# A decoder layer with expert retrieval: split products for the first block, two heads beside the last projection, another order at the close of blocks 2 and 1

## The chip, the cores and the metric

The kernel runs on one core of one Trainium2 chip. The metric is device time in microseconds (us) of one launch. The kernel before took 1467.91 us (median of 3 runs, 1463.35 to 1468.68). A measurement of it can tell about 0.5% from no change.

## The reference, cut to what matters

A layer on 512 tokens of width 1024, in float32: one projection to q, k, v of two groups of eight heads (dilated windows "a", stick-breaking "b"), an output projection, a layer norm, then a retrieval of 128 single-neuron experts per token out of 16384, and a second norm.

```python
def hybrid_mixer(x, w_in, w_out):
    proj = x @ w_in                       # (512,1024) @ (1024,3072)
    qa, ka, va, qb, kb, vb = split(proj)
    oa = dilated_window_attention(rotary(qa), rotary(ka), va)
    ob = stick_breaking_attention(qb, kb, vb)
    return concat(oa, ob) @ w_out

def stick_breaking_attention(q, k, v):    # per block of 128 queries
    z = q @ k.T * scale
    later = exclusive_reverse_cumsum(where(causal, log_sigmoid(-z), 0))
    return where(causal, exp(log_sigmoid(z) + later), 0) @ v

def peer_ffn(x, ...):                     # 128 experts per token
    idx, gates = top_k_of_products(x)
    act = gates * gelu(x . expert_u[idx])
    return act @ expert_v[idx]

x = layer_norm(alpha * x + hybrid_mixer(x))
x = layer_norm(alpha * x + peer_ffn(x))
```

## The kernel before

The tokens stand in four blocks of 128, tb = 0 to 3. Block 0 goes first by itself, so that its experts can be fetched while the other blocks are still in the mixer; blocks 1 to 3 follow together.

**Block 0.** `project_block0` (L247) runs over six groups of output columns (`GROUPS`, L225: kA, half of v, qA, kB, qB, the other half of v), four weight tiles of 512 KB each. A tile lands in one of four buffers (`WBUF`, name `w`) of the pool `wst` from SP's queue, and is multiplied in plain float32 (L267). Its heads, `four_a` (L423 to L439) and `four_b` (L447 to L462), four heads to a call, are written out by hand between the projection's steps, in a `manual_schedule` block: there each engine gets its instructions in the order of the code. `first_out`, `normalize`, `query_first` and the routing follow.

**Gathers.** With the routing of a block known, 128 rows of an expert table, one per token, are fetched by an indirect DMA that POOL issues (L792), 512 KB each. On DVE one pass forms the dot products (L801, into `hg`) for table u, or adds the scaled rows (L812) for table v. After the last u row of a block comes a Gelu on ACT (L803), which needs another function table than Exp and Ln do.

**The mixed stage.** `project_in` (L280) computes all six groups for blocks 1 to 3 with split products: `wload` copies a weight tile rounded to fp32r on ACT (`high`, L120), takes the remainder on DVE (`low`, L124), and `mm3` (L126 to L129) adds three fp32r products in place of one float32 product. These steps, the gathers (`early`, the first `PRE0` = 72) and the dilated heads of blocks 1 to 3 (`heads_a`) are interleaved in the ratio `MIXB` = (6, 4, 4): six gathers, four projection steps, four head steps. Here a scheduler of the tile framework sets the order.

**The stick-breaking heads.** A loop written by hand runs over 24 tasks, the heads of block 3, then 2, then 1. `head_b` has steps: scores and mask (L352, L354), exponentials on ACT (L358, L360), a running product on DVE (L362), the cumulative sum as a matmul (L364, L366), the last exponential (L368), output (L372). In each pass the loop steps three heads, takes two or three gathers (`take`), and moves a generator `fill` twice: the output projection of the block before (`project_out`, L550) and its norm (`normalize`, with transposes L173 and copies L578). After the loop it finishes what is left in `after` (closing of a block's heads) and `fill`, then runs `project_out(1)`, `normalize(1)`, the queries and the routing of blocks 1 to 3.

**The rest.** Blocks 2 and 3 compute with all experts' weights streamed from memory by SP (L910 and L1207 on PE), while the gathers for blocks 0 and 1 go on.

## Time and profile before

| what | value |
|---|---|
| median of the runs | 1467.91 us |
| the profiled execution's own time | 1464.93 us |
| its span | 1463.2 us |
| mean granted clock of PE | 0.974 of full |
| PE busy | 1364.4 us, 93% |
| DVE busy | 1198.9 us, 82% |
| ACT busy | 514.4 us, 35% |
| POOL busy | 689.6 us, 47% |
| bytes moved | 495.92 MB, 339 GB/s on average |

The page cuts the span into 40 slices of 36.6 us. The first 1.5 slices hold block 0's projection and heads, slices 4 to 8 the mixed stage, slices 9 to 12 the stick-breaking heads and the closing of blocks 2 and 1, the next three the queries and the routing, and the rest the streamed experts and the tail. A row of the timeline gives start, duration, engine, line, what is written and read, the number of instructions in the row, and in brackets the idle time ahead of it with what ended that time. A matmul's end is modelled, so rows of PE overlap by some tenths of a microsecond.

### The profile page before, as it was taken

What the parts mean: (1) busy time and instruction counts of PE and PEld (TensorE: products, weight loads), DVE (VectorE), ACT (ScalarE), POOL (GpSimd) and SP (SyncE); (2) the same over time, 40 slices, a digit from 0 to 9 for tenths busy, and PEclk for the clock granted to TensorE, in tenths of its full rate; (3) what the DMA queues carried; (4) which work ended last, traced back from release to release, by engine and by line L of the source; (5) the groups of instructions that cost most, each with busy time, mean ns of one, the idle gap of its engine ahead of it and who ended that gap; (6) DMA issues with size and microseconds to landing.
All of it is one profiled execution on the core that took longest, in us unless ns stands there. A gap on an engine that the chain in (4) does not pass through costs nothing.

```text
span 1463.2 us, 19573 instructions
## 1 busy us (share of the span) xinstructions
PE 1364.4 (93%) x6642; PEld 1110.5 (76%) x6642; DVE 1198.9 (82%) x2459; ACT 514.4 (35%) x1029; POOL 689.6 (47%) x526
## 2 busy tenths in 40 slices
PE   8997989999989997788899999999999999999796
PEld 4676877767659996667688888888888888888575
DVE  1259989778789999999988877878777887788887
ACT  1322444364422111699922222222222222222342
POOL 0002577677554332104566665555555565556200
PEclk9999999999889999899999999999999999999998
DMA  8778899899889988659899999999999999999872
GB/s 297 257 268 282 305 347 315 297 385 346 282 305 374 328 287 300 222 178 310 277 389 410 409 410 409 410 409 410 409 409 410 409 409 410 409 409 399 332 246 87
DMA packets 162579, 495.92 MB, mean 339 GB/s; under 512 B 15376, under 2 KB 47520, under 8 KB 162480
## 3 DMA queue, kind: packets, MB, share of 16 engines
q0 software_dynamic: 74304, 270.13, 49.1%
q1 hardware_dynamic: 86448, 218.92, 40.7%
q10 hardware_dynamic: 1728, 5.64, 1.0%
q8 instruction: 52, 0.85, 0.2%
q14 instruction: 47, 0.39, 0.1%
HBM read 477.78 MB, written 16.84 MB: 338 GB/s over the span
## 4 chain that ended last, share of the span: by engine, by line
PE 37%; DMA 26%; DVE 25%; issue 7%; ACT 4%; POOL 2%; SPq 0%; DVEq 0%; POOLq 0%; ACTq 0%
DMA g<-peer_v,eidx 15%; PE y L1207 9%; PE h L910 9%; DMA g<-peer_u,eidx 8%; DVE x L812 3%; DVE yg L812 3%; PE m L267 2%; POOL g L792 2%; DVE o L867 2%; PE m L550 2%; PE tr L550 1%; ACT o L876 1%; DVE vl L124 1%; DMA v<-peer_v 1%; DVE g L801 1%
## 5 line engine op out<-in xcount | busy, mean ns | idle before, releaser
L792 POOL DMA_INDIRECT g<-peer_u,eidx x256 | 349.4, 1365 | 325.5 <-DVE topi L597 123.8
L792 POOL DMA_INDIRECT g<-peer_v,eidx x256 | 334.3, 1306 | 348.1 <-DVE x L812 111.4
L910 PE MATMUL h<-xf,w 128*128 128x256 f32 x2048 | 474.0, 380 | 0.0
L910 PEld LDWEIGHTS h<-xf,w 128*128 128x128 f32 x2048 | 384.1, 191 | 52.2
L801 DVE SCALAR_TENSOR_TENSOR g<-g,x 128x1024 f32<-128x1024 f32 x256 | 305.3, 1221 | 44.8 <-DMA g<-peer_u,eidx 44.4
L1207 PE MATMUL y<-vh,a 128*128 128x512 f32 x928 | 287.6, 414 | 9.3 <-ACT a L1193 8.9
L1207 PEld LDWEIGHTS y<-vh,a 128*128 128x128 f32 x928 | 175.1, 190 | 49.7 <-ACT a L1193 11.4
L812 DVE SCALAR_TENSOR_TENSOR x<-g,hg,x 128x1024 f32<-128x1024 f32 x128 | 164.1, 1282 | 24.4 <-DMA g<-peer_v,eidx 23.9
L812 DVE SCALAR_TENSOR_TENSOR yg<-g,hg,yg 128x1024 f32<-128x1024 f32 x126 | 161.6, 1283 | 25.2 <-DMA g<-peer_v,eidx 24.6
L124 DVE TENSOR_TENSOR vl<-v,vh 128x1024 fp32r<-128x1024 f32 x122 | 148.8, 1221 | 36.4 <-ACT vh L1162 36.4
L902 ACT ACTIVATE gl<-h 128x256 f32<-128x256 f32 x128 | 48.6, 380 | 297.3 <-PE h L910 297.2
L1207 PE MATMUL y<-vl,a 128*128 128x512 f32 x464 | 146.4, 397 | 1.1 <-DVE vl L124 1.1
L1162 ACT ACTIVATE vh<-v 128x1024 fp32r<-128x1024 f32 x122 | 128.5, 1053 | 36.0 <-DMA v<-peer_v 18.7
L1207 PEld LDWEIGHTS y<-vl,a 128*128 128x128 f32 x464 | 87.3, 189 | 22.3 <-DVE vl L124 2.5
L1193 ACT ACTIVATE a<-gl 128x512 fp32r<-128x512 f32 x58 | 36.4, 627 | 178.8 <-DVE gl L1187 178.7
L876 ACT ACTIVATE o<-o1b,sg 128x128 f32<-128x128 bf16 x256 | 83.5, 400 | 3.4 <-DVE o1b L861 3.2
L882 PEld LDWEIGHTS m<-o,o 128*128 128x128 f32 x304 | 37.7, 191 | 20.9 <-ACT o L876 18.0
L882 PE MATMUL m<-o,o 128*128 128x128 f32 x304 | 41.7, 280 | 11.8 <-ACT o L876 7.6
L267 PE MATMUL m<-w,x0f 128*128 128x256 f32 (+1 forms) x128 | 45.5, 505 | 5.3 <-DMA w<-w_in 5.1
L128 PE MATMUL m<-wl,x2h 128*128 128x512 f32 x96 | 38.8, 404 | 8.3 <-DVE wl L124 8.3
L867 DVE TENSOR_TENSOR o<-sg,c_small 128x512 f32<-128x512 f32 x64 | 43.7, 683 | 2.4 <-PE a L882 2.2
L1186 DVE TENSOR_TENSOR gl<-gl,gt 128x480 f32<-128x480 f32 x64 | 41.8, 652 | 0.0
(297 smaller groups left out, 1815.5 us busy)
## 6 DMA issues: line engine op xcount, KB each, us to landing
w<-uT SPq DMA_DIRECT2D x128, 512.0 KB, 8.5
v<-peer_v SPq DMA_DIRECT2D x128, 512.0 KB, 7.3
w<-w_in SPq DMA_DIRECT2D x47, 512.0 KB, 4.7
gt<-gd SPq DMA_DIRECT2D x15, 960.0 KB, 11.6
w<-peer_wq SPq DMA_DIRECT2D x16, 512.0 KB, 4.6
wq<-peer_wq SPq DMA_DIRECT2D x16, 512.0 KB, 7.5
gd<-stage SPq DMA_DIRECT2D x15, 512.0 KB, 5.2
gd<-stage SPq DMA_DIRECT2D x15, 448.0 KB, 3.9
```

What stands on the lines that cost most here:

```text
L124: nc.vector.tensor_sub(parts[1], src, parts[0].bitcast(F32))
L267: nc.tensor.matmul(ps[:, ch * wd:(ch + 1) * wd], x0f[:, kk], w[:, k], start=kk == 0, stop=kk == KD - 1)
L792: nc.gpsimd.indirect_dma_start(out=u, out_offset=None, in_=a["peer_v" if kind else "peer_u"], in_offset=bass.IndirectOffsetOnAxis(ap=eidx[ ...
L801: nc.vector.scalar_tensor_tensor(u, u, 1.0, x, op0=OP.mult, op1=OP.mult, accum_out=hs[:, j:j + 1])
L812: nc.vector.scalar_tensor_tensor(acc, u, hs[:, j:j + 1], acc, op0=OP.mult, op1=OP.add)
L867: nc.vector.tensor_tensor(hot2[s], gate[tb][1][:, 0, t:t + TG, None].to_broadcast([P, TG, P]), iota[:, None, :].to_broadcast([P, TG, P]), ...
L876: nc.scalar.activation(hot[s][:, j], o1b[:, :, j], AF.Copy, scale=gate[tb][1][:, 1, t + j:t + j + 1])
L882: nc.tensor.matmul(gps[s][:, j * P:(j + 1) * P], o2[:, j], o1[:, j], start=True, stop=True)
L902: nc.scalar.activation(gls[c // 2][:, c % 2], ps[:, :ND], AF.Gelu)
L910: nc.tensor.matmul(hps[c][:, :ND], us[c][:, k], xf[:, k], start=k == 0, stop=k == KD - 1)
L1162: nc.scalar.activation(vsp[c][0], vs[c], AF.Copy)
L1207: nc.tensor.matmul(yps[t][hf], s_, w_[:, hf * 512:(hf + 1) * 512], start=c == 0 and n == 0, stop=c == P - 1 and n == len(terms) - 1)
```

## The change

Four things change. `project_block0` splits the weights of groups 1 to 5 as `wload` does, and block 0's tokens, and multiplies with `mm3`; group 0 stays in plain float32. The splits come two tiles ahead of their use, and their results stand in the buffers of `wsp` or in those that later hold the other blocks' tokens. The two transposed groups come from a new copy of their columns in memory, `w_t`, in 512-wide tiles. The mixed stage runs five groups; the sixth goes into a new block by hand together with the first two stick-breaking heads and eight gathers, and the ratio is (7, 4, 3) with 80 gathers. The loop over heads starts two passes later; after it the closing steps and the projection of block 1 stand ahead of the transposes of block 2. After the Gelu of block 0 the table that holds both Exp and Ln is loaded.

The diff:

```diff
@@ -73,8 +73,9 @@
 TG = 4
 LEAD = 30
 KT = 6
-MIXB = (6, 4, 4)
-PRE0 = 72
+MIXB = (7, 4, 3)
+PRE2 = 8
+PRE0 = 80
 QGATH = 3
 QH = 2
 PRE1 = 7
@@ -245,26 +246,59 @@
         turn(scaled(tb, kind, scale, ps), dst)
 
     def project_block0():
-        late = {}
+        late, raw, cut = {}, {}, {}
         n = 0
+        tiles = [(g, i) for g in range(len(GROUPS)) for i in range(4)]
+        flat = [x_.rearrange("p k t -> p (k t)") for x_ in (xh, xl)]
+        x0p = [x_[:, :D].rearrange("p (k t) -> p k t", k=KD) for x_ in flat]
+
+        def fetch(m):
+            if m >= len(tiles):
+                return
+            g, i = tiles[m]
+            w = raw[m] = wst.tile([P, 2, 512], F32, name="w", bufs=WBUF)
+            src = a["w_t"][g - 3, i] if GROUPS[g][0] == "t" else a["w_in"][g, i]
+            src = src.rearrange("p (k c) -> p k c", k=2)
+            if m == 0:
+                for k in range(2):
+                    (nc.scalar, nc.sync)[k].dma_start(w[:, k], src[:, k])
+                    (nc.sync, nc.scalar)[k].dma_start(x0f[:, 2 * k:2 * k + 2], a["x0T"][:, 2 * k:2 * k + 2])
+                nc.sync.dma_start(x0f[:, 4:], a["x0T"][:, 4:])
+            else:
+                nc.sync.dma_start(w, src)
+
+        def split(m):
+            if not 4 <= m < len(tiles):
+                return
+            w = raw.pop(m)
+            if m % 4 > 1:
+                parts = [x_[:, (m % 4 - 1) * D:(m % 4) * D].rearrange("p (k c) -> p k c", k=2) for x_ in flat]
+                nc.scalar.activation(parts[0], w, AF.Copy)
+            else:
+                parts = high(wsp, w, [P, 2, 512], "w")
+            low(w, parts)
+            cut[m] = parts
+
+        for m in range(2):
+            fetch(m)
         for g, (kind, _, scale) in enumerate(GROUPS):
             dst = target(g, 0)
             ps = bank("mm")
-            wd, kn = (256, 4) if kind == "t" else (512, 2)
             for i in range(4):
-                ch, kq = (i // 2, i % 2) if kind == "t" else (0, i)
-                w = wst.tile([P, kn, wd], F32, name="w", bufs=WBUF)
-                src = a["w_in"][g, i].rearrange("p (k c) -> p k c", k=kn)
-                if g == i == 0:
-                    for k in range(2):
-                        (nc.scalar, nc.sync)[k].dma_start(w[:, k], src[:, k])
-                        (nc.sync, nc.scalar)[k].dma_start(x0f[:, 2 * k:2 * k + 2], a["x0T"][:, 2 * k:2 * k + 2])
-                    nc.sync.dma_start(x0f[:, 4:], a["x0T"][:, 4:])
-                else:
-                    nc.sync.dma_start(w, src)
-                for k in range(kn):
-                    kk = kn * kq + k
-                    nc.tensor.matmul(ps[:, ch * wd:(ch + 1) * wd], x0f[:, kk], w[:, k], start=kk == 0, stop=kk == KD - 1)
+                fetch(n + 2)
+                split(n + 2)
+                for k in range(2):
+                    kk = 2 * i + k
+                    if g == 0:
+                        nc.tensor.matmul(ps, x0f[:, kk], raw[n][:, k], start=kk == 0, stop=kk == KD - 1)
+                    else:
+                        mm3(ps, x0p[0][:, kk], x0p[1][:, kk], cut[n][0][:, k], cut[n][1][:, k], kk == 0, kk == KD - 1)
+                if n in (1, 2):
+                    sl = slice(4 * n - 4, 4 * n)
+                    nc.scalar.activation(x0p[0][:, sl], x0f[:, sl], AF.Copy)
+                    nc.vector.tensor_sub(x0p[1][:, sl], x0f[:, sl], x0p[0][:, sl].bitcast(F32))
+                raw.pop(n, None)
+                cut.pop(n, None)
                 n += 1
                 if n in late:
                     turn(*late.pop(n))
@@ -277,10 +311,11 @@
             else:
                 late[n + (2 if kind == "rot" else 1)] = scaled(0, kind, scale, ps), dst
 
-    def project_in():
+    def project_in(groups):
         tbs = PARTS[1]
         n = len(tbs)
-        for g, (kind, _, scale) in enumerate(GROUPS):
+        for g in groups:
+            kind, _, scale = GROUPS[g]
             dst = target(g, 1)
             pst = None if kind == "t" else [bank("mm") for _ in range(n)]
             wd, kn = (256, 4) if kind == "t" else (512, 2)
@@ -571,6 +606,8 @@
         for sl in halves:
             nc.vector.scalar_tensor_tensor(r[:, sl], r[:, sl], rs, t[1][:, sl], op0=OP.mult, op1=OP.add)
         yield
+        if tb > 1:
+            yield
         for g in range(2):
             tr = transpose4(r[:, g * 512:(g + 1) * 512], "a" if g and tb == 0 else "tr")
             ks = slice(4 * g, 4 * g + 4)
@@ -801,6 +838,8 @@
             nc.vector.scalar_tensor_tensor(u, u, 1.0, x, op0=OP.mult, op1=OP.mult, accum_out=hs[:, j:j + 1])
             if j == P - 1:
                 nc.scalar.activation(hs, hs, AF.Gelu)
+                if tb == 0:
+                    nc.scalar.preload_act_table_set("natural_log_exp_and_others")
                 nc.vector.tensor_scalar_mul(x, x, ALPHA)
             return
         if j == 0:
@@ -933,7 +972,7 @@
         if out is not None:
             gelu(out, hps.pop(out))
 
-    proj = project_in()
+    proj, last = project_in(range(5)), project_in((5,))
     xload = load_x2()
     with tc.manual_schedule():
         def go(steps, n=1):
@@ -993,7 +1032,32 @@
     early = gathers(PRE0)
     until(mix(route_steps(0, 4, 4), head(early, PRE1), (2, 1)), proj, 1)
     run(head(early, 12), head(proj, 8), (3, 2))
-    run(early, proj, chain(*(heads_a(tb, rest) for tb in PARTS[1])), MIXB)
+    run(head(early, PRE0 - PRE1 - 12 - PRE2), proj, chain(*(heads_a(tb, rest) for tb in PARTS[1])), MIXB)
+
+    tasks = [("b", tb, h) for tb in (3, 2, 1) for h in range(NH)]
+    NTASK = len(tasks)
+    live, sts_, after = {}, {}, []
+
+    def begin(j):
+        kind, tb, h = tasks[j]
+        if h == 0:
+            sts_[tb] = group(tb)
+        live[j] = head_b(tb, h, sts_[tb], ("a", "b", "m0", "m1")[j % 4])
+
+    def go(j):
+        if 0 <= j < NTASK:
+            next(live[j])
+
+    with tc.manual_schedule():
+        order = [(0, 0), (), (0,), (1, 1), (), (), (), ()]
+        for todo in order:
+            for j in todo:
+                if j not in live:
+                    begin(j)
+                go(j)
+            next(last)
+            next(early, None)
+        run(last, early)
     qws.close()
     rqs.close()
     xf = open_pool(ctx, "xfp", "right").tile([P, KD, 2 * P], F32, name="xf")
@@ -1026,23 +1090,14 @@
             for _ in head(gs, n):
                 pass
 
-        tasks = [("b", tb, h) for tb in (3, 2, 1) for h in range(NH)]
-        NTASK = len(tasks)
-        live, sts_, after = {}, {}, []
         fill = iter(())
         lo_ = load_out()
-        for i in range(-1, NTASK + 2):
-            def go(j):
-                if 0 <= j < NTASK:
-                    next(live[j])
-
+        run(head(lo_, 2))
+        for i in range(1, NTASK + 2):
             next(lo_, None)
             new = i + 1 < NTASK
             if new:
-                kind, tb, h = tasks[i + 1]
-                if h == 0:
-                    sts_[tb] = group(tb)
-                live[i + 1] = head_b(tb, h, sts_[tb], ("a", "b", "m0", "m1")[(i + 1) % 4])
+                begin(i + 1)
                 go(i + 1)
             go(i)
             for g_ in list(after):
@@ -1050,11 +1105,13 @@
                     after.remove(g_)
             if new:
                 go(i + 1)
-            next(fill, None)
+            if i <= NTASK:
+                next(fill, None)
             go(i - 1)
             go(i - 1)
-            take(3 if 10 <= i < 18 else 2)
-            next(fill, None)
+            take(3 if 10 <= i < 18 or 18 <= i < NTASK and i % 2 else 2 if i <= NTASK else 0)
+            if i <= NTASK:
+                next(fill, None)
             if i >= 2:
                 go(i - 2)
                 kind, tb, h = tasks[i - 2]
@@ -1066,10 +1123,10 @@
                 for c in range(3):
                     load_u(c)
         for g_ in after:
-            for _ in g_:
-                take(2)
-        for _ in fill:
-            pass
+            next(g_)
+            next(fill)
+            next(g_)
+        take(1)
         qs.close()
         up = open_pool(ctx, "up", "left")
         qls = ExitStack()
@@ -1077,7 +1134,11 @@
         rq = open_pool(qls, "rq", "left")
         tops(PARTS[1])
         load_q(0)
-        for _ in project_out(1):
+        po1 = project_out(1)
+        for _ in head(po1, 4):
+            take(1)
+        run(fill)
+        for _ in po1:
             take(1)
         norm = normalize(1)
         next(norm)
@@ -1312,6 +1373,7 @@
         "xT": x.T.reshape(KD, P, S).transpose(1, 0, 2),
         "x0T": x[:P].T.reshape(KD, P, P).transpose(1, 0, 2),
         "w_in": np.stack([by_tile(f["w_in"].reshape(D, 6, 512)[:, g], g) for g in (1, 2, 0, 4, 3, 5)]),
+        "w_t": np.stack([f["w_in"].reshape(4, 2, P, 6, 512)[:, :, :, g].transpose(0, 2, 1, 3).reshape(4, P, 1024) for g in (4, 3)]),
         "w_out": f["w_out"].reshape(4, 2, P, 2, 512).transpose(3, 0, 2, 1, 4),
         "peer_wq": f["peer_wq"].reshape(2, 4, P, 8, 256).transpose(2, 3, 0, 1, 4),
         "skT": f["peer_sub_keys"].reshape(16, P, P).transpose(2, 0, 1),
```

How this moves instructions is seen at three places. The first is ACT in block 0's projection, from the second turned group on; `su` are the heads' score rows, `x2h` and `wh` copies of weight tiles. Before:

```order
L223 ACTIVATE qA_181<-tr 128x512
L429 ACTIVATE su<-su 128x512 x2
L236 ACTIVATE q<-m_227 128x512
L223 ACTIVATE kB<-tr 128x4x128
L435 ACTIVATE su<-a 128x512
L435 ACTIVATE su<-b 128x512
```

With the change, on the same engine and at the same place:

```order
L276 ACTIVATE x2h<-w 128x1024 x2
L224 ACTIVATE qA_225<-tr 128x512
L464 ACTIVATE su<-su 128x512 x2
L121 ACTIVATE wh<-w 128x1024 x2
L237 ACTIVATE q<-m_299 128x512
L276 ACTIVATE x2h<-w 128x1024
L224 ACTIVATE kB<-tr 128x4x128
L470 ACTIVATE su<-a 128x512
L276 ACTIVATE x2h<-w 128x1024
L470 ACTIVATE su<-b 128x512
```

The copies of weight tiles 16 and 17 (`wh`, x2) now stand right behind the exponentials of the dilated heads' scores (L464, which was L429).

The second place is DVE at the end of the mixed stage, where the projection's last remainders (`wl`), the gathers' passes (`g,hg`) and the first running product of the stick-breaking heads (`su<-a,su`) meet. Before:

```order
L378 TENSOR_TENSOR o<-h,rz 128x512
L801 SCALAR_TENSOR_TENSOR g_2168,hg<-g_2168,x_100 128x1024
L801 SCALAR_TENSOR_TENSOR g,hg<-g,x_100 128x1024 x4
L124 TENSOR_TENSOR wl<-w,wh 128x1024 x2
L801 SCALAR_TENSOR_TENSOR g,hg<-g,x_100 128x1024
L801 SCALAR_TENSOR_TENSOR g_2227,hg<-g_2227,x_100 128x1024
L801 SCALAR_TENSOR_TENSOR g_2230,hg<-g_2230,x_100 128x1024
L801 SCALAR_TENSOR_TENSOR g,hg<-g,x_100 128x1024 x2
L124 TENSOR_TENSOR wl<-w,wh 128x1024
L801 SCALAR_TENSOR_TENSOR g,hg<-g,x_100 128x1024 x2
L362 SCALAR_TENSOR_TENSOR su<-a,su 128x512
```

With the change:

```order
L412 RECIPROCAL rz<-z 128x8
L413 TENSOR_TENSOR o<-h,rz 128x512
L125 TENSOR_TENSOR wl<-w,wh 128x1024
L838 SCALAR_TENSOR_TENSOR g,hg<-g,x_100 128x1024 x2
L397 SCALAR_TENSOR_TENSOR su<-a,su 128x512
L125 TENSOR_TENSOR wl<-w,wh 128x1024
L838 SCALAR_TENSOR_TENSOR g,hg<-g,x_100 128x1024
L838 SCALAR_TENSOR_TENSOR g_2313,hg<-g_2313,x_100 128x1024
L397 SCALAR_TENSOR_TENSOR su<-b,su 128x512
L838 SCALAR_TENSOR_TENSOR g,hg<-g,x_100 128x1024
L125 TENSOR_TENSOR wl<-w,wh 128x1024
```

The first running products (L362, now L397) have moved from behind the last remainder to between the four remainders of the last group. Ahead of the last remainder stand 79 gathers' passes, where there were 72; ahead of the streamed experts' first remainder 240, where there were 238.

The third place is PE at the close of the loop over heads: the last head's cumulative sum (`c_tri`, `mones`) and output (`h<-v,su`), the transposes of block 2's normalized rows (`x_100`) and of the closed heads (`o`), and block 1's output projection (`wo`). Before:

```order
L364 MATMUL m_3044<-su,c_tri 128x256
L366 MATMUL m_3044<-su,mones 128x128
L372 MATMUL h<-v,su 128x64 x2
L173 MATMUL tr<-c_ident,x_100 128x128 x8
L372 MATMUL h<-v,su 128x64 x2
L173 MATMUL tr<-c_ident,o 128x128 x4
L550 MATMUL m_3181<-wo_2381,x_2357 128x512 x2
L550 MATMUL m_3181<-wo_2411,x_2357 128x512 x2
```

With the change:

```order
L399 MATMUL m_3197<-su,c_tri 128x256
L401 MATMUL m_3197<-su,mones 128x128
L407 MATMUL h<-v,su 128x64 x4
L174 MATMUL tr<-c_ident,o 128x128 x4
L585 MATMUL m_3307<-wo_2561,x_2537 128x512 x2
L585 MATMUL m_3307<-wo_2563,x_2537 128x512 x2
L585 MATMUL m_3307<-wo_2565,x_2537 128x512 x2
L585 MATMUL m_3307<-wo_2597,x_2537 128x512 x2
L174 MATMUL tr<-c_ident,x_100 128x128 x8
L585 MATMUL tr<-wo_2625,x_2537 128x512 x2
```

The eight transposes of block 2 have moved from between the last head's outputs to the middle of block 1's output projection.

## The prediction

> **What bounds the kernel now.** I read the slices of the page first, to see which engine is full in which stage; then the windows by stage; then the waits of the stages where the engines are not full; and last the timeline of those places. The slices are 36.6 us each.
>
> ```profile
> span 1463.2 us, 19573 instructions
> PE   8997989999989997788899999999999999999796
> DVE  1259989778789999999988877878777887788887
> PEclk9999999999889999899999999999999999999998
> GB/s 297 257 268 282 305 347 315 297 385 346 282 305 374 328 287 300 222 178 310 277 389 410 409 410 409 410 409 410 409 409 410 409 409 410 409 409 399 332 246 87
> ```
>
> From slice 21 on DMA moves 409 to 410 GB/s without a break: that is the second half, where the experts' weights stream. The first half has no such ceiling. One window of the middle and one of the second half show the two limits:
>
> ```profile
> 475.00:500.00 25.00, 25.00 (x157) 23.10 (x157) 25.00 (x96) 3.11 (x7) 9.72 (x11) 1.00 0.93 327
> 750.00:775.00 25.00, 25.00 (x114) 21.23 (x114) 20.94 (x23) 6.37 (x10) 16.53 (x12) 1.00 1.03 410
> PE y L1207 <- ACT a L1193: 0.7, 1, 0.7
> ```
>
> The columns are PE, PEld, DVE, ACT and POOL busy, then clock, DMA share and GB/s. At 475 us PE and DVE are both full. At 750 us PE is full at full clock and DMA is saturated; the third row is the longest wait for data that PE has from 745 to 1340 us, 0.7 us. So nothing ahead of 450 us is absorbed later: the change touches what runs up to about 440 us, and a microsecond gained or lost there moves the end by a microsecond, except that the gathers left over for later cost DVE and DMA time of their own (part G). All terms below stand against the profiled run, 1464.9 us, 3 us under the median of 1467.9 of the runs shown.
>
> **A, block 0's projection.** What the change speeds up is the matmul of a weight tile:
>
> ```profile
> 18.34 13.92 PE L267 MATMUL m<-w,x0f 128*128 128x512 f32 x40
> 81.76 0.40 PE L128 MATMUL m<-wl,x2h 128*128 128x512 f32 x1
> 81.99 0.40 PE L129 MATMUL m<-wh,x2l 128*128 128x512 f32 x1
> ```
>
> The first row is tiles 6 to 13 of the block's 24: 13.92 us, less the 0.17 us by which a modelled end stands over, is 1.72 us a tile. Split products follow each other every 0.23 us (81.76 to 81.99); six make a tile, 1.37 us. Twenty tiles are split, 20 x 0.35 = 7 us if PE alone set the pace. It does not. A raw tile now holds its buffer through its transfer, an ACT copy and a DVE subtraction:
>
> ```profile
> w<-w_in SPq DMA_DIRECT2D x24, 512.0 KB, 4.6
> L120 ACT ACTIVATE wh<-w 128x1024 fp32r<-128x1024 f32 x24 | 25.4, 1058 | 43.1 <-PE m L129 39.0 <-PE m L128 3.9
> L124 DVE TENSOR_TENSOR wl<-w,wh 128x1024 fp32r<-128x1024 f32 x24 | 29.2, 1219 | 0.3 <-ACT wh L120 0.3
> ```
>
> 4.6 + 1.06 + 1.22 = 6.9 us over four buffers is 1.72 us a tile, just what the f32 matmul took. So PE idles 0.35 us a tile instead of working, and nothing is gained while the stream of tiles sets the pace. Behind this stands the order: on ACT and DVE the splits are queued among the dilated heads' operations, and the split of tile 16 comes after the heads' last row:
>
> ```profile
> 33.38 0.82 PE L423 MATMUL a<-kA,qA 64*128 64x128 f32 x5 [0.69 <-ACT qA L223]
> 34.58 0.69 DVE L426 TENSOR_TENSOR su<-a,c_maska 128x512 f32<-128x512 f32 x1 [4.22 <-PE a L423]
> 40.84 0.69 DVE L430 TENSOR_REDUCE z<-su 128x4 f32<-128x512 f32 x1 [0.70 <-ACT su L429]
> 39.02 1.89 PE L267 MATMUL m<-w,x0f 128*128 128x256 f32 x8
> 59.87 1.02 PE L457 MATMUL a<-su,c_tri 128*128 128x512 f32 x2
> ```
>
> The heads' chain runs from 34.58 to 41.5 us (both shifted by about 0.7, since the scores start at 34.1). In front of it DVE waited 4.22 us and nobody cared; now PE's next tile is behind it. Tile 16 started at 39.02; I have it at 42.3. From there to the end of tile 23 (59.87) took 20.9 us, of which split products save some 3: 42.3 + 20.9 - 3 = 60.2, and the clock falls to half behind a gap of 4 us (part D shows the case), which costs another 2 to 3. **A: +3**, between -7 (all of the matmul gain) and +6 (no gain, and the gap and the clock in full).
>
> A page speaks against this part. The Trainium skill, "TensorE: Matmul & The Clock Gate", section "Architectural detail", says that ACT and DVE run their queues strictly in order; so a subtraction behind a head's reduction cannot overtake it, and the sum by that rule is the +3; were the splits free to overtake, it would be the -7. No row here shows an overtaking.
>
> **B, the mixed stage up to the end of the projection of blocks 1 to 3.** A round holds one weight tile; it had six gathers and now has seven, with three head steps instead of four. The last group moves behind the dilated heads, into a block with the first two stick-breaking heads and eight of the gathers. The order on SP stays as it was, so these weights are fetched as early as before; on POOL the eight gathers are issued between the group's tiles.
>
> ```profile
> 195.00 1.22 DVE L124 TENSOR_TENSOR wl<-w,wh 128x1024 fp32r<-128x1024 f32 x1
> 207.17 1.22 DVE L124 TENSOR_TENSOR wl<-w,wh 128x1024 fp32r<-128x1024 f32 x1
> 202.58 1.22 DVE L801 SCALAR_TENSOR_TENSOR g<-g,x 128x1024 f32<-128x1024 f32 x1
> 203.73 1.22 DVE L801 SCALAR_TENSOR_TENSOR g<-g,x 128x1024 f32<-128x1024 f32 x1
> 196.00:292.00 96.00, 91.59 (x494) 70.99 (x494) 81.73 (x162) 39.23 (x88) 65.41 (x46) 0.98 0.89 313
> 291.93 0.39 PE L129 MATMUL m<-wh,x2l 128*128 128x512 f32 x1
> ```
>
> A round takes 12.2 us (195.00 to 207.17), a gather on DVE 1.15 us (202.58 to 203.73). By the instruction order 79 gathers instead of 72 stand ahead of the last subtraction: 7 x 1.15 = 8.1 us more DVE work before the end of the projection, which was at 292.2. DVE is busy 81.7 of 96 us in this stage, so at most 14.3 us are there to take it; PE is idle 4.4 us. Lower end -4: PE's idle time goes. Upper end +8: no cover, because the heads that are left run their chains without projection work beside them and the last group's splits wait behind two heads' rows. DVE at 85% is nearer to the upper end: **B: +6**. These gathers come back in part E and G, where they are no longer to be done.
>
> **C, the start of the stick-breaking heads.** The first head had nothing beside it:
>
> ```profile
> 297.81 1.12 PE L364 MATMUL a<-su,c_tri 128*128 128x512 f32 x2 [2.31 <-DVE su L362]
> 300.00:305.00 5.00, 5.00 (x21) 3.67 (x20) 5.00 (x11) 3.20 (x6) 4.08 (x4) 0.76 1.02 412
> ```
>
> 2.31 us of waiting, some 0.7 us just before it, and a quarter of 5 us lost to the clock: 4.2 us. Now that head's scores and exponentials lie under the last group's matmuls. **C: -4**, 0 if the group itself waits there.
>
> **D, normalizing block 3.** The transposes move one step later, so that they no longer stand on PE ahead of their input:
>
> ```profile
> 372.51 0.66 PE L173 MATMUL tr<-c_ident,x 128*128 128x128 f32 x4 [1.66 <-DVE x L572]
> 373.85 0.96 PE L173 MATMUL tr<-c_ident,x 128*128 128x128 f32 x4 [0.69 <-ACT xf L578]
> 375.00:380.00 5.00, 5.00 (x20) 4.36 (x20) 5.00 (x11) 2.74 (x6) 4.09 (x4) 0.50 0.69 215
> 380.00:385.00 5.00, 5.00 (x23) 4.28 (x22) 3.14 (x6) 2.19 (x6) 3.02 (x4) 0.57 0.95 336
> 384.68 1.94 PE L550 MATMUL m<-wo,xf 128*128 128x512 f32 x4
> ```
>
> The two waits are 2.35 us; the clock of 0.50 and 0.57 behind them loses 2.5 + 2.15 = 4.65 us. Together 7.0; but DVE is full in 375 to 380 too and sets a floor, so I count five of them: the next output projection starts at 379.5 instead of 384.68. **D: -5**, between 0 and -7.
>
> **E, closing blocks 2 and 1.** PE now runs half of block 1's output projection while DVE normalizes block 2, whose transposes come after it.
>
> ```profile
> 405.12 0.56 PE L372 MATMUL h<-v,su 128*128 128x64 f32 x4
> 405.73 1.28 ACT L161 ACT_TABLE_LOAD   x1
> 410.35 1.11 PE L173 MATMUL tr<-c_ident,x 128*128 128x128 f32 x4 [4.67 <-DVE x L572]
> 412.15 1.12 PE L173 MATMUL tr<-c_ident,x 128*128 128x128 f32 x4 [0.69 <-ACT xf L578]
> 414.70 1.11 PE L173 MATMUL tr<-c_ident,o 128*128 128x128 f32 x4 [0.69 <-ACT o L383]
> 410.00:415.00 5.00, 3.28 (x14) 2.69 (x15) 5.00 (x6) 1.79 (x3) 2.28 (x2) 0.50 0.06 6
> 415.61 8.44 PE L550 MATMUL m<-wo,x 128*128 128x512 f32 x16
> 423.88 7.03 PE L550 MATMUL tr<-wo,x 128*128 128x512 f32 x16
> ```
>
> Waits of 4.67 + 0.69 + 0.69 = 6.05 us go; PE's 3.28 us of work at clock 0.50 would be 1.6, and the first half of the projection took 8.44 where the second half, at full clock, 7.03: 1.6 + 1.4 = 3 more. Sum 9. Against it: the tail of the last head (scores to output) still has some 2 us without ordinary matmuls, and half a clock behind it costs 2 to 4. The table loads, four of 1.28 us, lie in these chains on ACT; kept tables take them out, and they are counted in the waits. **E: -7**, between -3 and -10. What is late next is DVE, which from here on is full.
>
> A rule bears on it. The Trainium skill, "TensorE: Matmul & The Clock Gate", sections "HAM oscillation" and "Part 4: PE-mode transpose", allows gaps up to about 3.4 us and does not count transposes as work. The trace agrees as far as it goes: 371 to 374.6 us, 3.6 us with transposes only, was followed by 0.50. By that rule the 2 us at the tail cost nothing and E would be -9.
>
> **G, gathers left.** By the order two gathers fewer remain when the second half begins. A gather's 0.52 MB at 410 GB/s is 1.28 us (an estimate from the rate row); PE is bound there too. **G: -1**, between 0 and -2.6.
>
> **The sum**: 3 + 6 - 4 - 5 - 7 - 1 = -8, that is 1464.9 - 8 = **1457 us**, from 1450 to 1463 with the smaller errors of C to G.
>
> **Rivals.** *R1, the split pays in full:* transfers land faster than 4.6 us, or the heads' rows fit between the splits. For it: PE's work does fall by 7 us, and DVE and ACT are mostly idle up to 34 us. Against it: 1.72 us a tile from the buffers. A = -7, the sum -18: 1447. *R2, the front eats the gains:* A = +6 and B = +8, the sum -3 by themselves; with C at 0, because the last group waits beside the first heads, +1: 1462 to 1466. For it: DVE's 85%, and the strictly interleaved order. Against: the idle 14.3 us. *R3, slower:* block 0's PE stays at half clock from tile 14 to 23. At half clock a split tile takes 2.74 us against 1.72: 10 x 1.02 = 10 us, and the heads' own matmuls between them (9 us busy) add 5 to 9: +15 to +19 on the forecast, 1472 to 1476. It decides if gaps like that before tile 16 repeat in each group; a gap of 0.7 us (33.38) did not do it, one of 3.6 us did, and I expect one long gap only. That the table would be loaded again anyway is ruled out by the order, where no loads stand between the heads' exponentials.
>
> **How the numbers follow.** Forecast 1457: 0.50. R1 0.17, R2 0.25, R3 0.08. The range takes in R1 with its bounds and R2, and leaves out R3 and the far end of R1: 1443 to 1469. Against the median, 0.5%, about what a measurement of this kernel can tell from no change, is 7.3 us, so faster means under 1460.6: R1 and four fifths of the forecast, 0.57. Within 0.5%: R2 and the rest, 0.35. Slower: R3, 0.08.
>
> **What would show it.** A: tile 23's matmuls end at 61 to 63 us (R1: by 54), with a gap of about 4 us around 40 and waits for the splits on PE. B: the last split product of the projection ends near 298 (R1 and a good B: 292 or less). C and D: no waits of over 1 us for DVE at the start of the heads and after block 3's projection, and the clock above 0.9 there. E: the output projection of block 1 starts about 13 us earlier than 415.6, and PE's wait for block 2's normalized rows is gone. G: the second half's windows are the same. Wrong it would be if DVE's queue, not PE's, sets the stages C to E: then the gathers moved ahead show up as DVE time without a gap, and the gains of C to E shrink to the 2 us of G.

## The result, and the profile after

The changed kernel took 1485.31 us (median of 4 runs, 1481.0 to 1486.97) against 1466.01 us before (4 runs): a ratio of 1.0127, with a 95% interval of 1.0096 to 1.0158. It is slower by some 19 us, where 1457 was forecast. Its profiled execution took 1486.97 us, with a span of 1485.1 us.

The same slices of the page as before, now 37.1 us each:

```profile
span 1485.1 us, 19664 instructions
PE   7998989889989999588899999999999999999896
DVE  4459998556898999999998777877778887788888
PEclk9899998679999999799999999999999999999998
GB/s 299 205 277 284 302 367 343 247 138 382 316 339 347 335 314 309 206 226 260 297 329 410 410 408 410 410 410 409 409 410 410 409 410 409 410 410 401 351 249 91
```

Slices 8 and 9 (260 to 334 us) stand out: the clock falls to 0.6 and 0.7, DVE to 5 tenths, DMA to 247 and 138 GB/s, where there were 297 and 385. PE's row hardly shows it, with 8 tenths busy in both. Four places in the two traces, all starts on PE or POOL, tell where the time went:

| from ... to | before, us | after, us | difference | forecast |
|---|---|---|---|---|
| start to the first gather | 128.4 | 133.4 | +5.0 | A: +3 |
| to the projection's last product | 163.5 | 200.0 | +36.4 | B: +6 |
| to the first cumulative sum | 5.9 | 1.5 | -4.4 | C: -4 |
| to the first product of the queries | 132.9 | 123.3 | -9.6 | D and E: -12 |
| to the end of the span | 1032.5 | 1026.9 | -5.5 | G: -1 |

The rows at both ends of these stretches that stand nowhere else here, of before and then of the changed kernel:

```profile
128.39 1.00 POOL L792 DMA_INDIRECT g<-peer_u,eidx  x1 [123.76 <-DVE topi L597]
430.75 3.62 PE L653 MATMUL a<-xf,wq 128*128 128x256 f32 x16
```

```profile
133.44 0.99 POOL L829 DMA_INDIRECT g<-peer_u,eidx  x1 [128.80 <-DVE topi L634]
458.18 3.62 PE L690 MATMUL a<-xf,wq 128*128 128x256 f32 x16
```

So in this profile all terms but one came out within 5 us of the forecast; the mixed stage, B, lost 36 us in place of 6. A second profile of the changed kernel (e11_change_again, below) has 130.7, 196.7, 1.5, 129.3 and 1028.7 us for the same stretches: B lost 33 us there too, but D and E gained 3.6 us only. A difference of a few microseconds in one profile is therefore not yet a finding.

The windows of 275 to 325 us, of before and then of the changed kernel (PE, PEld, DVE, ACT, POOL busy, clock, DMA share, GB/s):

```profile
275.00:300.00 25.00, 20.57 (x95) 15.24 (x94) 18.63 (x31) 10.09 (x16) 17.73 (x14) 0.98 0.88 301
300.00:325.00 25.00, 25.00 (x139) 19.19 (x138) 20.45 (x36) 14.70 (x25) 18.38 (x16) 0.95 1.02 409
```

```profile
275.00:300.00 25.00, 21.44 (x64) 13.32 (x65) 8.62 (x21) 7.43 (x17) 9.12 (x7) 0.53 0.49 170
300.00:325.00 25.00, 20.72 (x76) 15.76 (x76) 12.30 (x19) 8.29 (x11) 6.48 (x4) 0.70 0.33 107
```

From 275 to 300 us PE is as busy as before with two thirds of the instructions, at a clock of 0.53 instead of 0.98; everything else waits. What PE does there, in the changed kernel's timeline (L363 are a dilated head's scores, L373 its transposes, L379 its output, L128 to L130 the projection):

```profile
285.73 1.11 PE L373 MATMUL a<-c_ident,su 128*128 128x128 f32 x4
287.59 1.97 PE L379 MATMUL h<-v,su 128*128 128x64 f32 x8 [0.75 <-ACT su L376]
289.49 2.07 PE L363 MATMUL a<-kA,qA 64*128 64x512 f32 x2
291.49 1.11 PE L373 MATMUL b<-c_ident,su 128*128 128x128 f32 x4
293.35 1.97 PE L379 MATMUL h<-v,su 128*128 128x64 f32 x8 [0.75 <-ACT su L376]
...
307.70 0.80 PE L128 MATMUL m<-wh,x2h 128*128 128x512 f32 x1 [1.34 <-ACT wh L121]
...
333.40 0.39 PE L130 MATMUL m<-wh,x2l 128*128 128x512 f32 x1
...
334.87 1.08 PE L399 MATMUL a<-su,c_tri 128*128 128x512 f32 x2
```

Between the fifth group's last product (271 us) and the sixth group's first (307.70) there is almost nothing but dilated heads of block 3, one after the other (the scores of the first stick-breaking head come at 301 us). A head comes every 5.76 us (287.59 to 293.35): 1.97 + 2.07 + 1.11 us of PE work at half clock, whose modelled ends overlap a little, and 0.75 us until ACT has copied. With three head steps per round instead of four, six of the 24 heads were left when the five groups were through; and the sixth group, which could have covered them, stood in a block behind them. POOL's timeline shows that the gathers stopped as well:

```profile
310.32 1.68 POOL L829 DMA_INDIRECT g<-peer_u,eidx  x1 [24.37 <-DVE g L838]
```

By 286 us the 72 passes that the stage has on DVE were done and 79 gathers issued; the last eight passes, which free the buffers for more gathers, are in that block too.

### The profile page after: what moved, and what is told of

Same layout as the page of the kernel before. It is cut to its first block, busy times and chain, and to the rows that moved or that the text cites. A ratio compares the mean times of both kernels' runs of the same rounds, so it can differ in the third digit from the quotient of the medians.

```text
span 1485.1 us, 19664 instructions
## 1 busy us (share of the span) xinstructions
PE 1381.3 (93%) x6650; PEld 1126.7 (76%) x6650; DVE 1222.9 (82%) x2481; ACT 530.8 (36%) x1047; POOL 694.5 (47%) x526
## 4 chain that ended last, share of the span: by engine, by line
PE 67%; DVE 17%; DMA 5%; issue 5%; ACT 3%; POOL 1%; SPq 0%; DVEq 0%; ACTq 0%; POOLq 0%
PE h L949 24%; PE y L1268 21%; PE a L690 3%; PE b L690 3%; DVE g L838 2%; DVE o L906 2%; DMA v<-peer_v 2%; DVE x L851 1%; PE m L129 1%; DVE yg L851 1%; PE m L130 1%; DMA w<-w_in 1%; PE m L128 1%; ACT o L915 1%; PE h L658 1%
## 5 line engine op out<-in xcount | busy, mean ns | idle before, releaser
L1223 ACT ACTIVATE vh<-v 128x1024 fp32r<-128x1024 f32 x122 | 128.4, 1053 | 32.1 <-DMA v<-peer_v 15.2
L129 PE MATMUL m<-wl,x2h 128*128 128x512 f32 x116 | 49.8, 429 | 9.1 <-DVE wl L125 8.8
L128 PE MATMUL m<-wh,x2h 128*128 128x512 f32 x116 | 49.5, 431 | 4.6 <-ACT wh L121 4.6
L121 ACT ACTIVATE wh<-w 128x1024 fp32r<-128x1024 f32 x34 | 35.5, 1056 | 37.9 <-PE m L130 17.8
L130 PE MATMUL m<-wh,x2l 128*128 128x512 f32 x116 | 48.4, 417 | 0.0
```

What stands on the lines that cost most here:

```text
L128: nc.tensor.matmul(ps, ah, bh, start=first, stop=False, **kw)
L129: nc.tensor.matmul(ps, ah, bl, start=False, stop=False, **kw)
L1223: nc.scalar.activation(vsp[c][0], vs[c], AF.Copy)
```

## The experiments

Each run is compared with the kernel before on its own chip; the runs came in four groups on three chips (the second and third group on the same one), and before's median there was 1463.8, 1463.9, 1465.1 and 1464.0 us.

**Are the left-over heads the cause?** Two ways to cover them, and the split undone beside them.

```diff
 e1_ratio4
-MIXB = (7, 4, 3)
+MIXB = (7, 4, 4)
 e2_group5_in_mix
-    proj, last = project_in(range(5)), project_in((5,))
+    proj, last = project_in(range(6)), project_in(())
...
-            next(last)
+            next(last, None)
 e3_block0_f32
 (project_block0 as it was before the change)
```

> The change with one number put back: four head steps per round instead of three, so that all 24 dilated heads stand among the first five groups' matmuls and none is left over (six were, all of block 3). Theory T1 (the left-over heads ran alone, six times 5.8 us): about 33 us less than the changed kernel's 1485, that is about 1452. Rival T2 (the block with the last group beside two heads is itself what costs, by waits for its splits): over 1475.

> The change with the sixth group put back into the mixed stage; the ratio (7, 4, 3) stays, the two first heads keep their block but have no matmuls of the projection beside them. T1: the six heads are covered by the sixth group's 72 products; some 30 us less, less what the uncovered first heads cost (4 us): about 1456. T2 also expects a gain. A rival T3 (three heads a round slow the whole stage, wherever the group stands): over 1475.

> The change with block 0's projection put back to plain float32 products; all else stays. The split costs what the traces show at the end of its projection (59.9 us before, 65.5 after): 5 to 6 us less than the changed kernel, about 1480. Rival: the delay is absorbed by the waits behind it (the output weights' transfer, the routing), within 1 us of the changed kernel.

Measured: e1_ratio4 1465.84 us, ratio 1.0008 (0.9987 to 1.0029); e2_group5_in_mix 1464.92 us, 0.9996 (0.9973 to 1.0019); e3_block0_f32 1480.29 us, 1.0084 (1.0057 to 1.0111). Either way of covering the heads takes 19 to 20 us off the changed kernel (17 to 19 by the ratios): T1 holds, and T3 (three heads a round slow the stage wherever the group stands) falls with the second run, which has three. T2, as the whole cause, falls with the first run, which keeps the last group's block. But both expected 1452 to 1456, 10 us less. In e1_ratio4 the projection ends at 311.8 us instead of 333.4, not at 292, and its trace shows that PE stands in the block of the last group, so that T2 keeps a part:

```profile
284.87 0.53 PE L128 MATMUL m<-wh,x2h 128*128 128x512 f32 x1 [2.16 <-ACT wh L121]
288.07 0.80 PE L129 MATMUL m<-wl,x2h 128*128 128x512 f32 x1 [2.67 <-DVE wl L125]
300.40 0.51 PE L128 MATMUL m<-wh,x2h 128*128 128x512 f32 x1 [0.92 <-ACT wh L121]
302.46 0.79 PE L129 MATMUL m<-wl,x2h 128*128 128x512 f32 x1 [1.55 <-DVE wl L125]
...
311.78 0.39 PE L130 MATMUL m<-wh,x2l 128*128 128x512 f32 x1
```

The group's weight copies wait on ACT behind the two heads' exponentials, and the remainders on DVE behind gathers: 7.3 us of waits. The split of block 0 costs about 5 us in the changed kernel (1485.3 to 1480.3; ratios 1.0127 and 1.0084, with intervals that overlap).

**The closing and the table.** The kernel before with the closing order alone, and with the table alone; later both together, twice.

```diff
 e4_close_only (the kernel before, with)
+        if tb > 1:
+            yield
...
         for g_ in after:
-            for _ in g_:
-                take(2)
+            next(g_)
+            next(fill)
+            next(g_)
...
+        for _ in head(po1, 4):
+            take(1)
+        run(fill)
 e5_table_only (the kernel before, with)
+                if tb == 0:
+                    nc.scalar.preload_act_table_set("natural_log_exp_and_others")
 e10_close_table, e15_close_table_again: both
```

> The kernel before with the closing alone: the transposes of blocks 3 and 2 a step later, closing steps and half of block 1's projection ahead of block 2's transposes, a third gather in some passes. As predicted (D and E): 12 us less than before, about 1454. By the changed kernel's trace (from the last head's output to the queries 21.3 us instead of 25.1): 4 us less, about 1462. Rival: the gathers taken in earlier passes give it back on DVE, no difference.

> The kernel before with the table of Exp and Ln loaded right behind block 0's Gelu, and nothing else. Theory: of four loads of 1.28 us only the two at 405.7 and 407.2 lie in a chain for which PE waits, so 1 to 3 us less than before. Rival: DVE, not ACT, ends that wait, no difference.

> The kernel before with the two parts that did no harm alone: the closing order and the kept table. If the parts add up (0.997 and 0.9994): a ratio of 0.996 to 0.997, some 5 us under before on the same chip. If the kept table matters only where the closing waits: the same as the closing alone, 0.997.

> The run with closing and table only, once more, as the measure for the two runs before it on the same chip: a ratio to before of 0.995 to 0.997.

Measured: closing alone 1460.07 us, 0.997 (0.9944 to 0.9995); table alone 1464.38 us, 0.9994 (0.9967 to 1.0021), no difference; both 1460.42 us, 0.9952 (0.9924 to 0.9981), and again 1459.86 us, 0.9962 (0.9936 to 0.9988). The pair is the version that beats both kernels, by 4 to 5 us against before, a good third of the 12 that D and E were to bring. First closing alone, then both (e10_close_table), at the last head's output:

```profile
407.70 1.28 ACT L161 ACT_TABLE_LOAD   x1
...
409.96 1.28 ACT L162 ACT_TABLE_LOAD   x1
...
412.00 1.12 PE L173 MATMUL tr<-c_ident,o 128*128 128x128 f32 x4 [3.60 <-ACT o L383]
412.90 9.49 PE L550 MATMUL m<-wo,x 128*128 128x512 f32 x16
```

```profile
408.31 0.66 PE L173 MATMUL tr<-c_ident,o 128*128 128x128 f32 x4 [1.11 <-issue]
408.80 7.03 PE L550 MATMUL m<-wo,x 128*128 128x512 f32 x16
```

In the first trace the copy `o` for which PE waits stands on ACT behind the norm's two table loads: a wait of 3.60 us, and then 9.49 us for 16 products. In the second no load stands there, the wait is 1.11 us and the same products take 7.03. But the wait differs as much between traces that all keep the table. Here are the second profile of the pair (e15_close_table_again) and the one of e14_split_alone (closing, table and split, below):

```profile
400.16 0.90 PE L173 MATMUL tr<-c_ident,o 128*128 128x128 f32 x4 [1.81 <-ACT o L383]
```

```profile
405.50 0.20 ACT L161 ACTIVATE lw<-lw 128x1 f32<-128x1 f32 x1 [5.24 <-DVE lw L160]
...
406.48 1.12 PE L173 MATMUL tr<-c_ident,o 128*128 128x128 f32 x4 [5.51 <-ACT o L416]
```

In the last one ACT has no load to do; the norm's first step on it (`lw`) waits 5.24 us for DVE, which first works off five of the gathers' passes, from 397.6 to 403.6 us. So the traces do not show what the kept table adds to the closing, and in time the intervals of 0.997 and of the pair overlap as well.

**Covered heads without the split, and copies ahead of the exponentials.**

```diff
 e6_ratio4_f32: e1_ratio4 and e3_block0_f32 together
 e7_copies_first: e6_ratio4_f32, with
-        order = [(0, 0), (), (0,), (1, 1), (), (), (), ()]
+        order = [(), (0, 0), (), (0,), (), (1, 1), (), ()]
```

> The change with four head steps per round and block 0 in plain float32: what is left of it is the block of the last group beside two heads, the closing and the table. T1 plus the measured cost of the split: 5 us less than the run with four head steps alone (1465.8), about 1461, that is 2 to 3 us under the kernel before of the same chip. If split and left-over heads shared one delay, no less than 1465.

> As the run before, and in the block of the last group the copies of its weight tiles are issued ahead of the two heads' exponentials on ACT (first tile ahead of head 0, third tile ahead of head 1). Theory T2 (in this block the copies wait in ACT's queue behind exponentials that wait for PE's scores, and PE waits for the copies: 2.2 + 2.7 and 0.9 + 1.6 us in the run with four head steps, with a falling clock behind each): 7 to 10 us less than the run before, 1451 to 1454. Rival: DVE with its gathers ends those waits, within 2 us of the run before.

Measured: 1466.03 us, 1.0021 (0.9998 to 1.0044), and 1470.53 us, 1.005 (1.0026 to 1.0074). Both expectations missed. Undoing the split showed no gain here: the trace has the first gather 2.2 us earlier than e1_ratio4's (129.5, 131.7) and the projection's end at the same 312.0 us. And the copies put ahead made it slower; the longest wait moved to DVE, and the four waits of the block add up to 8.4 us instead of 8.0:

```profile
287.20 0.79 PE L129 MATMUL m<-wl,x2h 128*128 128x512 f32 x1 [5.35 <-DVE wl L125]
```

So T2, with ACT's queue as the cause, falls: the rival named there, DVE with its gathers, ends the longest of these waits, though the run is 4.5 us slower where that rival had allowed 2.

**The clock of the left-over heads.** Work is added to the changed kernel (T3 in the texts of these runs is the theory of the half clock):

```diff
 e8_extra_matmuls, e12_extra_again
+        if tb == 3 and h > 1:
+            extra = bank("mm")
+            for k in range(8):
+                nc.tensor.matmul(extra[:, :3 * P], xh[:, k, :P], xh[:, k], start=k == 0, stop=k == 7)
```

> The change with work added: behind the scores of block 3's last six dilated heads, eight fp32r matmuls of 128x384 each that nothing reads. Theory T3 (the left-over heads run at half clock although PE is busy 85 to 95% there, because transposes and narrow float32 products do not hold the clock up): the added matmuls raise the clock, a head falls from 5.8 us towards 3.5, and the time falls by up to 9 us in spite of 48 added instructions, about 1476. Rival (the clock follows the gaps, or the heads' chain has its length at any clock): 5 to 10 us more, 1490 to 1495.

> The changed kernel itself, once more, as the measure for the next run on the same chip: a ratio of 1.0127 to before, within its interval.

> The run with 48 added matmuls once more, beside the changed kernel on one chip. T3: in its profile the six left-over heads went by every 3.1 to 3.5 us instead of 5.8, at full clock, and the projection ended at 317.6 instead of 333.4; if that carries through, 5 to 12 us less than the changed kernel here. Rival: the first pair of runs was two chips apart, and the two are the same within 2 us.

Measured: the first time 1479.96 us, 1.0117 (1.0084 to 1.0149), too near to the changed kernel's ratio to tell; then both on one chip, the changed kernel 1486.6 us, 1.0131 (1.0088 to 1.0174), and with the added products 1479.74 us, 1.0091 (1.0056 to 1.0126): 7 us less with 48 instructions more, though the intervals overlap. In the profiles of that pair the projection's last product starts at 321.0 us instead of 327.5, and the first product of the queries at 451.4 instead of 458.2, which is the difference in time. The left-over heads of the first of these runs, and its window of 280 to 290 us:

```profile
281.81 1.10 PE L383 MATMUL h<-v,su 128*128 128x64 f32 x8 [0.40 <-ACT su L380]
...
285.30 1.10 PE L383 MATMUL h<-v,su 128*128 128x64 f32 x8 [0.75 <-ACT su L380]
```

```profile
280.00:290.00 10.00, 8.34 (x51) 5.85 (x49) 2.09 (x6) 4.67 (x10) 0.00 (x0) 1.00 0.18 70
```

The same head takes 3.5 us instead of 5.76, at full clock, with PE less busy (8.34 of 10 us) than in the changed kernel at half clock (9.25). The added products stood ahead of these heads and not beside each of them: the last began at 281.1 us. The second run with them shows what follows when they are over; there the last began at 285.0:

```profile
285.74 1.10 PE L383 MATMUL h<-v,su 128*128 128x64 f32 x8 [0.40 <-ACT su L380]
289.23 1.10 PE L383 MATMUL h<-v,su 128*128 128x64 f32 x8 [0.75 <-ACT su L380]
290.93 1.11 PE L377 MATMUL b<-c_ident,su 128*128 128x128 f32 x4
293.20 1.92 PE L383 MATMUL h<-v,su 128*128 128x64 f32 x8
```

Some 6 us behind the last added product the transposes take 1.11 us instead of 0.66, and the same output 1.92 instead of 1.10: the clock has halved, with no idle time of PE over 0.75 us in between.

**Gathers.** The mixed stage and the last group with fewer gathers:

```diff
 e9_fewer_gathers: e6_ratio4_f32, with
-MIXB = (7, 4, 4)
-PRE2 = 8
-PRE0 = 80
+MIXB = (6, 4, 4)
+PRE2 = 0
+PRE0 = 72
```

> The change with block 0 in float32, the ratio (6, 4, 4) and 72 early gathers as before, none of them in the block of the last group. Theory T4 (in that block, and ahead of it, the gathers' passes on DVE stand in front of the remainders for which PE waits): the projection ends some 8 to 10 us earlier than the 312 us of the run with four head steps and float32; the eight gathers are done later at about 1.2 us each on DVE, so the time falls by 0 to 4 us against that run (ratio to before 0.999 to 1.002). Rival T2 (the two heads' exponentials in ACT's queue alone hold the group up): the projection still ends near 310.

Measured: 1478.71 us, 1.009 (1.0063 to 1.0117), 13 us more than e6_ratio4_f32 (10 by the ratios), where up to 4 less were expected. The projection did end earlier, at 305.3 us instead of 312.0, and the queries began at 430.2 instead of 438.6, as early as in the kernel before. But the block of the last group kept its wait for DVE, which grew to 9.44 us although the order has no gathers in it: DVE works off nine passes of the gathers ahead of it, one after another from 270.44 us on, before the first remainder.

```profile
282.02 0.80 PE L129 MATMUL m<-wl,x2h 128*128 128x512 f32 x1 [9.44 <-DVE wl L125]
```

What the queries had gained, and more, was lost behind them: eight gathers fewer stood ahead of the streamed experts, and POOL had them to do there. Groups of POOL from 745 us on, of before and of this run:

```profile
L792 POOL DMA_INDIRECT g<-peer_v,eidx x137 | 190.2, 1388 | 129.5 <-DMA g<-peer_v,eidx 54.8 <-DVE x L812 16.9 <-issue 16.5
```

```profile
L796 POOL DMA_INDIRECT g<-peer_v,eidx x143 | 198.4, 1387 | 132.3 <-DMA g<-peer_v,eidx 62.8 <-issue 20.3 <-DVE x L818 18.3
```

Six gathers more there, and the span behind the queries 1040.6 us against 1032.5. The profiles of e9_fewer_gathers and e6_ratio4_f32 account for 1.4 us of the difference between the two runs (spans of 1470.8 and 1469.4 us); the profiled execution was the fastest of the eleven of e9_fewer_gathers, and where the rest of the 10 to 13 us went is not seen. Over the profiles, by the gathers that the order has ahead of the streamed experts: 232 left 1040.6 us, 236 left 1034 to 1036 (the four runs with the closing on the kernel before), 238 left 1032 (the kernel before and the table alone), 240 left 1027 to 1031 (the changed kernel and all others). That is about 1.5 us a gather, near the 1.28 us that a gather's 512 KB would take at 410 GB/s by estimate.

**What keeps the rest from gaining.**

```diff
 e13_mix_f32: e2_group5_in_mix and e3_block0_f32 together
 e14_split_alone: e10_close_table with the changed project_block0
```

> The change with the sixth group back in the mixed stage and block 0 in float32; what is left is the closing, the table, the ratio and eight more early gathers. If the split's 5 us add up where no block of the last group absorbs them: a ratio of about 0.996 (0.9996 less 5 us). If not, it stays at 0.999 to 1.000, as the split made no difference beside the block of the last group.

> The kernel before with the closing order, the table and block 0's split products: against the run with closing and table only it differs by the split alone, in a kernel that leaves no head over. By the first gather of the traces (128.4 us before, 133.4 with the change): 4 to 6 us more than the next run. Rival: the mixed stage takes it up, the same within 1.5 us.

Measured: e13_mix_f32 1466.03 us, 1.0005 (0.9975 to 1.0036); e14_split_alone 1462.0 us, 0.9975 (0.9949 to 1.0001), 2.1 us above closing and table on the same chip. The intervals do not tell these 2 us of the split by itself from nothing. The first run has neither the split nor the last group beside the two heads, and still does not gain. Its window of 290 to 300 us:

```profile
290.00:300.00 10.00, 10.00 (x64) 8.23 (x62) 0.69 (x1) 4.45 (x9) 0.00 (x0) 1.00 0.01 2
```

PE is full at full clock here, while DVE, POOL and DMA are empty: at seven to a round the last early gather is issued at 282.0, 15 us before the projection ends, and the first stick-breaking heads behind it are uncovered again (PE waits 3.36 us for DVE at 308.7).

## Why the prediction was wrong

**B is the step that failed.** It said of the upper end: "no cover, because the heads that are left run their chains without projection work beside them", and priced that with the gathers' passes on DVE, 8 us. The mechanism was named and the wrong thing was counted. The heads that are left cost their own length on PE: six heads, 36 us from 271 to 307, where seven passes of 1.15 us had been counted. The prediction says neither how many heads are left (six stand behind the fifth group's last product) nor what a head by itself takes. Even at full clock, at 3.5 us each, six would have been 21 us. Covering them takes 19 to 20 us off (e1 and e2), the whole loss against the kernel before. It is not all of B: with the heads covered, in e1_ratio4, the stretch still takes 180.0 us, 16.5 more than before and 10 more than forecast, of which 7.3 us are the waits in the last group's block. That part the upper end had in words ("the last group's splits wait behind two heads' rows") without a price of its own. The rival of the slower side, R3, had the clock as its mechanism, but in block 0, which was not it: the clock there was 0.83 from 35 to 65 us, and at half from 45 to 50 alone. That 1485 us is nearer to R3's 1472 to 1476 than to any other number of the prediction is chance.

**A** was +3 and came out at +5 by the trace and by e3_block0_f32, and at 2 where no heads are left over (e14_split_alone). Over all traces it is near the forecast: the first gather starts at 131.4 us on the mean of the seven with the split, at 127.9 of the ten without. Its argument held: in the changed kernel's trace PE waits behind the heads' scores for the split of tile 16, and the clock is 0.50 from 45 to 50 us, behind the gap.

```profile
43.97 0.50 PE L128 MATMUL m<-wh,x2h 128*128 128x512 f32 x1 [1.74 <-ACT wh L121]
45.23 0.80 PE L129 MATMUL m<-wl,x2h 128*128 128x512 f32 x1 [0.76 <-DVE wl L125]
...
65.46 1.02 PE L492 MATMUL a<-su,c_tri 128*128 128x512 f32 x2
```

The scores began at 35.55 instead of the 34.1 expected, and tile 23 was through at 65.5, not 61 to 63. The 7 us of matmul time (R1) show in no run.

**C** was right in the trace, -4.4 between the projection's end and the first sum. It is not a gain of its own, though: the last group waits in the same block, 7.3 us in e1_ratio4.

**D and E** were -12 and came out at -9.6 between the first sum and the queries, and at -3.6 in the second profile; the first steps of two heads were only moved ahead of that stretch. On the kernel before, the closing order alone gave -3.8 us by the medians and with the table -4.2 and -4.7. The waits that were counted go, and others come in their place. In D, the transposes of block 3 wait 0.2 us for DVE instead of 1.66, but the second four of them then wait for ACT's copy `xf` of the first four, 1.07 and 3.12 us in the two profiles of the changed kernel where it was 0.69; in the second of them other heads' exponentials stand ahead of that copy. In E, the copy `o`, which PE now needs first, stands in ACT's queue behind the norm's logarithm and exponential, which wait for DVE. So the sign of being wrong that the prediction named for this stage, that DVE's queue sets it, did show in E. The changed kernel has the wait too:

```profile
439.52 0.66 PE L174 MATMUL tr<-c_ident,o 128*128 128x128 f32 x4 [2.61 <-ACT o L418]
440.01 8.73 PE L585 MATMUL m<-wo,x 128*128 128x512 f32 x16
```

**G** was -1 and was -5.5. The estimate took the gathers' bytes; the profiles of different counts give about 1.5 us for each, which would be 3 for two of them, and the second profile of the changed kernel has -3.8. The rest of the -5.5 is within the spread of the profiles with 240 gathers (1027 to 1031 us).

**What stays open.** With the heads covered, and without the split, the gain of closing and table (4 to 5 us) is not seen (e6_ratio4_f32, e13_mix_f32). The stretch of B is 182.6 and 168.1 us in their profiles, against 163.5 before; but six profiles of kernels whose code is the same in this stretch (before, e4, e5, e10, e14 and e15) spread from 158.6 to 169.3, so that one profile cannot place the second figure. The eight gathers more in the mixed stage, 9 us of DVE, are one candidate, and e9_fewer_gathers, which takes them out and is slower, speaks against it as the whole answer. The last group's block without any gather's pass ahead of its remainders on DVE was not tried.

## What to carry to other kernels

When a ratio of interleaved work is changed, count what is left of each stream when the shortest one ends, and price the leftover by its own chain alone, from scores to output, at the clock that it would have alone. A gather done earlier costs its pass where it is put (1.2 us of DVE here) and returns its share where it was (about 1.5 us of the span here), so price both sides; and measure the sum, since putting eight back cost 10 to 13 us where two profiles would have said 1.4. Where a copy becomes the first thing that PE needs, look at what stands ahead of it in its engine's queue, and at what that in turn waits for.

## What was not expected of the hardware

Two windows of the changed kernel, in the columns used above:

```profile
280.00:290.00 10.00, 9.25 (x25) 5.59 (x26) 2.55 (x6) 2.12 (x5) 4.72 (x5) 0.50 0.83 288
290.00:300.00 10.00, 8.51 (x24) 4.59 (x23) 1.60 (x5) 2.60 (x6) 0.00 (x0) 0.50 0.02 6
```

The clock of PE was at 0.50 from 280 to 300 us while PE was 85 to 93% busy by the profile, with no idle time over 0.75 us, in both profiles of the changed kernel. The work was transposes, float32 products with 64 columns of output, and float32 products over 64 rows. The fall itself, between 276 and 278 us, stands behind an idle time of 1.54 us in the changed kernel, so a gap could have set it off there. In the second run with added products it could not: with 48 fp32r products of 128x384, some 0.18 us each, the clock was at 1.00 until 290 us, and it halved some 6 us behind the last of them with idle times of 0.40 and 0.75 us only. In the first run with them the heads were still at full clock 7 us behind the last one (an output that began at 288.37 took 1.10 us), so these runs give no fixed delay. The Trainium skill, "TensorE: Matmul & The Clock Gate", section "HAM oscillation", speaks of idle gaps over about 3.4 us; here a stretch of narrow work was followed by the same fall. That transposes do not count, as its section "Part 4: PE-mode transpose" has it, fits with this; that narrow float32 products count little is what these runs suggest, without telling which of the kinds weighs how much.
